# One layer of a hybrid decoder trunk on one core: sums of squares ahead of the input projection, eight input buffers, and outer products without their priority

## The chip, the cores and the metric

The kernel runs on one core of one Trainium2 chip. The metric is the device time of one execution in microseconds. Three runs of the kernel before took 1131.49, 1137.46 and 1138.11 us; their median is 1137.46 us.

## The reference

One layer works on x of 1024 tokens by 1024 channels in float32, with a conditioning vector c. What the change touches is its beginning:

```python
c_act = jax.nn.silu(c)
mod = (c_act @ w_mod[l] + b_mod[l])[:, None, :]
sh1, sc1, g1, sh2, sc2, g2 = jnp.split(mod, N_MOD, axis=-1)
h = _rms(x, norm1_w[l]) * (1 + sc1) + sh1      # x * rsqrt(mean(x*x)) * weight
proj = h @ w_in[l]
u, q, k, v = jnp.split(proj, ...)
y_ssm = _s5(u, ...)        # state-space branch: 32 groups of 16 channels, scan over positions
y_attn = _swa_sink(...)    # attention in a sliding window of 128, with sinks
x = x + g1 * (concat(norm(y_ssm), norm(y_attn)) @ w_out[l])
...                        # norm, gated MLP with a convolution of width 3, second residual
```

The state-space branch is computed in blocks of 8 positions; its discretised matrices are outer products of per-group vectors with powers of the state matrix, and they depend on the parameters alone.

## The kernel before, in words

Channels lie on the 128 partitions, in 8 tiles (k = 0 to 7) of 128 channels by 1024 tokens. A float32 product is made of three products of a fast type: each operand is split into an upper part (ScalarE, `act.copy` or `act.activation`) and a lower part (VectorE, the difference), and `mm3` (L143) adds upper x upper, upper x lower and lower x upper in one bank of PSUM. There are 8 banks.

The first projection gives u, the 512 channels of the state-space branch, with the tokens sorted by their residue j modulo 8 (T = 8): bank j takes the tokens j, j+8, ... , and its 24 products run over the 8 tiles k. The norm's factor of a token is applied only when a bank is emptied (`u_out`, L277), so the products need no norm. For each k the loop at L239 to L264

- loads x's tile (four buffers, taken in turn), a tile of the modulation weights (`emit_mod`, L178) and every second time a tile of w_in,
- reduces the modulation weights against the activated c on VectorE (L180; the trace names it CUSTOM_DVE and gives it the line 180), and forms the scale `mods` (L249),
- splits w_in's tile into the parts in `wus`, and x times the scale into `hT[k]` (tHA, tHB, tH: upper part L251 on ScalarE, lower part L252 on VectorE),
- squares x on ScalarE (L254) and adds the squares over the partitions by a product with a matrix of ones into banks 6 and 7 (L258; each shows as two records in the trace),
- adds this k's part to the six banks 0 to 5.

Behind the loop `rsqrt_mean` (L187 to L192) turns banks 6 and 7 into the norm's factor `rstd`, four instructions on ScalarE and four on VectorE; eight products with a single column, two records each, bring it from a row into a column of bank 7 (L272), and L273 copies it to `rc`. `u_out` empties banks 0 to 5, partly on VectorE, and the residues 6 and 7 are computed in banks 6 and 0 (L285 to L288).

After that come eight more tiles of modulation weights (L293), from which the shift's operand `shs` is cast and split (L296, L297). `shift_u` (L299) multiplies it with all parts of w_in. On VectorE the parameters of the state-space branch are prepared meanwhile: exponentials, sines, powers of the state matrix (PWr, PWi), and then `outer` (L415): a product with PWr, a product with PWi and their sum, for four tiles `IB` (L430; first matrix) and for `CAt` (L437; second matrix). IB is made inside `tc.high_priority(0)`. TensorE transposes IB later (L531), applies it to u (L566) and hands it to VectorE, whose scan begins with two memsets (L578). Heads of q, k and v run through `head` (L510), with weights loaded and split in `head_w` (L459).

What stands where on an engine is settled when the program is built: a list scheduler with its own estimate of times puts each instruction in its engine's order, each engine works its order off strictly, and instructions under `pin` keep the order of the text on TensorE. DMAs are issued by SyncE (SP) in order, with eight semaphores in turn.

Of the kernel before, what the change touches and what calls it, by code (L numbers as in the profile page):

```python
# [12 lines left out]
AF = mybir.ActivationFunctionType  # L13
ALU = mybir.AluOpType
ADD, SUB, MUL, MAX, MIN = ALU.add, ALU.subtract, ALU.mult, ALU.max, ALU.min
# [4 lines left out]
T = 8  # L20
# [42 lines left out]
def hymba_kernel(ctx, tc, xT, c, wmod, wu, wkvq, small, consts, relb, pq, wglu, wout, wup, wdn, out):  # L63
# [4 lines left out]
    bank = [pp.tile([128, 512], F32, name=f"bk{i}") for i in range(8)]  # L68
    SIZES = {"HA": 2048, "HB": 2048, "S16": 4128, "XQ": 4096}

    def new(tag, dt=F32):
        return pool.tile([128, SIZES.get(tag, 1024)], dt, tag=tag, name="t" + tag)
# [11 lines left out]
    def newr(tag):  # L84
        return RT(new(tag, F32R))

    vec, act, pol, sync = nc.vector, nc.scalar, nc.gpsimd, nc.sync
# [38 lines left out]
    def stt(o, a, s, b, op0, op1):  # L126
        return vec.scalar_tensor_tensor(out=o, in0=a, scalar=s, in1=b, op0=op0, op1=op1)  # L127
# [9 lines left out]
    def split(x, src, hi_eng="a", lo_eng="v"):  # L137

        hi, lo = x
        cpy(hi_eng, hi.r, src)  # L140
        tt(ENG[lo_eng], lo.r, src, hi.f, SUB)

    def mm3(o, a, b, start, stop, chain=False):  # L143

        pe.matmul(o, a[0].r, b[0].r, start=start, stop=False, skip_group_check=chain)
        pe.matmul(o, a[0].r, b[1].r, start=False, stop=False, skip_group_check=chain)
        pe.matmul(o, a[1].r, b[0].r, start=False, stop=stop, skip_group_check=chain)

    def sl(x, cols):
        return x[0][:, cols], x[1][:, cols]  # L150
# [4 lines left out]
    def half(t):  # L155
        return t[:, 0:512], t[:, 512:1024]
# [5 lines left out]
    def S(name, j=0, n=None):  # L162
        o, w = SMALL[name]
        return sm[:, o + j:o + (w if n is None else j + n)]
# [3 lines left out]
    early = new("S16")  # L168
    cact = new("X7")
# [5 lines left out]
    mod = pool.tile([128, 48], F32, name="mod")  # L175
    mods = pool.tile([128, 16], F32, name="mods")

    def emit_mod(j, st, ca):  # L178
        sync.dma_start(out=st, in_=wmod[j])
        vec.tensor_tensor_reduce(  # L180
            out=st, in0=st, in1=ca, scale=1.0, scalar=S("b_mod", j, 1), op0=MUL, op1=ADD,
            accum_out=mod[:, j:j + 1],
        )
# [42 lines left out]
    n1s = pool.tile([128, 8], F32, name="n1s")  # L226
    ts(n1s, S("n1w"), -1.0, MUL)
    hT, wus = [], []
    for k in range(8):
        if k < 2:  # L230
            t_ = newr(("HA", "HB")[k])
# [2 lines left out]
            hT.append((newr(f"H{2 * k}"), newr(f"H{2 * k + 1}")))  # L234
    wux = newr("XQ")
    jt = new("A12")[:, 0:512]
    xs = [new("X4"), new("X5"), new("X6"), early[:, 3072:4096]]
    wst = None
    for k in range(8):  # L239
        xk = xs[k % 4]  # L240
        sync.dma_start(out=xk, in_=xT[k])
        emit_mod(8 + k, early[:, (k % 3) * 1024:(k % 3 + 1) * 1024], cact)
        if k % 2 == 0:
            wst = new(("W0", "A10")[k // 2 % 2])
            sync.dma_start(out=wst, in_=wu[k // 2])
        w = half(newr(f"U{k}") if k < 4 else wux[:, (k - 4) * 1024:(k - 3) * 1024])
        wus.append(w)
        split(w, wst[:, (k % 2) * 512:(k % 2) * 512 + 512])
        stt(mods[:, k:k + 1], mod[:, 8 + k:9 + k], 1.0, n1s[:, k:k + 1], ADD, MUL)  # L249
        hi, lo = hT[k]  # L250
        act.activation(out=hi.r, in_=xk, func=AF.Identity, scale=mods[:, k:k + 1])  # L251
        stt(lo.r, xk, mods[:, k:k + 1], hi.f, MUL, SUB)  # L252
        sq = new(("A11", "A1")[k % 2])
        act.activation(out=sq, in_=xk, func=AF.Square)  # L254
        if k == 0:
            sync.dma_start(out=cn, in_=consts[:, 0:384])
        for h in range(2):
            pe.matmul(bank[6 + h], ones, sq[:, h * 512:h * 512 + 512], start=(k == 0), stop=(k == 7))  # L258
        if k == 1:
            Q12, P12, Bs_t = new("W1"), new("U5"), new("U4")  # L260
            sync.dma_start(out=Q12, in_=pq[0])
            sync.dma_start(out=P12, in_=pq[1])
        for j in range(6):
            mm3(bank[j], sl(hT[k], slice(j, 1024, T)), w, k == 0, k == 7)  # L264
    rstd = new("X6")
    rc = pool.tile([128, 8], F32, name="rc")
    rtmp = new("A11")
# [3 lines left out]
    for j in range(T):  # L271
        pe.matmul(bank[7][:, j:j + 1], rstd[0:1, j:1024:T], ones[0:1, 0:1], start=True, stop=True)  # L272
    act.copy(rc, bank[7][:, 0:8])  # L273
    U = new("S16")[:, 0:4096]
    Uv = U.rearrange("p (g d h) -> p g d h", d=8, h=16)

# [5 lines left out]

    for j in range(6):
        u_out(j, bank[j])
    for j, b in ((6, bank[6]), (7, bank[0])):  # L285
        for k in range(8):
            mm3(b, sl(hT[k], slice(j, 1024, T)), wus[k], k == 0, k == 7)
        u_out(j, b)  # L288
# [139 lines left out]
        tt(eng, o, o, tmp, ADD)  # L428

    IB = [new(f"A{5 + i}") for i in range(4)]  # L430
    hp = ctx.enter_context(ExitStack())
    hp.enter_context(tc.high_priority(0))
    for i in range(4):
        tmp = new("A10") if i == 3 else IB[i + 1]
        outer(vec, IB[i], tmp, 8 * i, 8, 8, Bb, Bsw)
    hp.close()
    CAt = [new(f"A{i}") for i in range(5)]  # L437
    for i in range(4):
        outer(vec, CAt[i][:, 0:1008], CAt[i + 1][:, 0:1008], 7 * i, 7, 9, P1, P2)
# [170 lines left out]
    for i2 in range(2):  # L610
        b = abank()
# [10 lines left out]
    for q in range(4):  # L622
        sync.dma_start(out=kd[:, 8 * q:8 * q + 8, 112:240],
                       in_=ka[32 * q:32 * q + 16, :].rearrange("p (g x) -> p g x", x=128))
# [91 lines left out]
    for i in range(8):  # L716
        b = bank[int(pick("YB", i))]
# [11 lines left out]
    for m in range(4):  # L729
        zv = zT[m].rearrange("p (c t) -> p t c", t=8)  # L730
        for q2 in range(2):
            b = sbank()
# [632 lines left out]
```

## Time and profile before

| | |
|---|---|
| runs before, us | 1131.49, 1137.46, 1138.11 |
| median | 1137.46 |
| profiled execution | 1138.01 |
| its span (first to last instruction) | 1136.1 |
| TensorE matmul busy | 1050.8 us, 92% of the span |
| VectorE busy | 928.0 us, 82% |
| ScalarE busy | 581.0 us, 51% |
| GpSimd busy | 269.0 us, 24% |
| granted TensorE clock, mean over the span | 0.962 of full |

A share of busy time is a mean over stages with different limits, so it says little about one stage. In the rows below, times are in microseconds from the start of the span; a row of the order of time gives the start, the time from the first start to the last end, the engine, the source line, the operation, the tiles out<-in, shapes and the count, and in brackets the idle time before it and what ended it. Buffer numbers are left out: tH stands for several tiles. The granted clock is the share of full speed that TensorE was given; it has two levels, 1.2 and 2.4 GHz.

### The profile page before, as it was taken

The page shows a single profiled execution, that of the slowest core. Times are in us where ns is not written, and L with a number is a line of the kernel's source. Part 1 is how long each engine was busy: PE and PEld are TensorE (multiplying, and loading weights), DVE is VectorE, ACT ScalarE, POOL GpSimd, SP SyncE. Part 2 cuts the span into 40 slices and gives each one's busy share as a digit, 9 for nine tenths or more (in the row PEclk, how much of TensorE's full clock was granted, in tenths as well). Part 3 has the DMA queues.
Part 4 walks back from the last instruction along what each step waited for, and adds up shares of the span by engine and source line. Part 5 has one row for each costly group of instructions (what it writes and reads, how often), then busy time and mean ns, then how long its engine had stood idle before and what let it go on. Part 6 is the DMA issues. An engine that isn't in the chain of part 4 may idle for free.

```text
span 1136.1 us, 13319 instructions
## 1 busy us (share of the span) xinstructions
PE 1050.8 (92%) x4692; PEld 828.1 (73%) x4692; DVE 928.0 (82%) x1493; ACT 581.0 (51%) x1008; POOL 269.0 (24%) x153
## 2 busy tenths in 40 slices
PE   6989999579989899779999999999999979989998
PEld 4877777366556577657888888888888768768876
DVE  7994899949887587888777878797778797998985
ACT  5415443578895366736544545455444554434342
POOL 0000000011233102762222223212212143353541
PEclk9989999689999899979999999999999989999999
DMA  9501516014018855222223232423123359220002
GB/s 364 224 19 38 118 50 93 1 66 139 19 47 213 258 180 155 93 93 94 92 86 112 82 128 93 154 88 112 56 93 116 125 210 382 74 93 1 1 38 112
DMA packets 48487, 128.14 MB, mean 113 GB/s; under 512 B 6146, under 2 KB 14114, under 8 KB 48419
## 3 DMA queue, kind: packets, MB, share of 16 engines
q1 hardware_dynamic: 46114, 123.09, 31.8%
q0 software_dynamic: 2304, 4.20, 2.3%
q8 instruction: 37, 0.61, 0.2%
q14 instruction: 32, 0.25, 0.1%
HBM read 105.28 MB, written 21.99 MB: 112 GB/s over the span
## 4 chain that ended last, share of the span: by engine, by line
PE 44%; DVE 11%; ACT 1%; DMA 1%; issue 1%; SPq 0%; DVEq 0%; ACTq 0%
PE bk L97 43%; DVE tA L118 2%; DVE tH L118 2%; DVE tU L118 2%; PE bk L99 1%; DVE tXQ L127 1%; DVE tX L127 1%; DVE tXQ L118 1%; DVE tX L118 1%; DVE tS L118 1%; DMA tS<-in_dram 0%; DMA tX<-xd 0%; ACT tU L133 0%; DVE tHA L118 0%; DMA tW<-in_dram 0%
## 5 line engine op out<-in xcount | busy, mean ns | idle before, releaser
L97 PE MATMUL bk<-tA,tU 128*128 128x512 f32 x516 | 128.1, 395 | 0.8 <-DVE tA L118 0.8
L97 PE MATMUL bk<-tU,tU 128*128 128x512 f32 x516 | 123.4, 391 | 4.8 <-DVE tXQ L127 2.4
L97 PEld LDWEIGHTS bk<-tU,tU 128*128 128x128 f32 x516 | 96.5, 188 | 27.4 <-issue 2.8
L97 PE MATMUL bk<-tH,tU 128*128 128x512 f32 x477 | 115.9, 392 | 0.0
L97 PEld LDWEIGHTS bk<-tA,tU 128*128 128x128 f32 x516 | 96.7, 188 | 24.2 <-DVE tA L118 1.4
L127 DVE SCALAR_TENSOR_TENSOR tX<-tH,sm,tX 128x1023 f32<-128x1023 f32 x66 | 100.2, 1519 | 7.7 <-ACT tX L1100 7.6
L97 PEld LDWEIGHTS bk<-tH,tU 128*128 128x128 f32 x477 | 89.1, 188 | 19.2
L97 PE MATMUL bk<-tA,tXQ 128*128 128x512 f32 x300 | 74.5, 395 | 1.0 <-ACT tH L1053 1.0
L97 PE MATMUL bk<-tH,tA 128*128 128x512 f32 (+1 forms) x168 | 62.5, 502 | 10.6 <-ACT tH L133 6.5
L99 PE MATMUL bk<-tH,tU 128*128 128x512 f32 x267 | 65.8, 402 | 2.3 <-DVE tU L118 2.3
L97 PEld LDWEIGHTS bk<-tA,tXQ 128*128 128x128 f32 x300 | 56.3, 188 | 14.5 <-ACT tH L1053 1.4
L133 ACT CAST tU<-tW 128x512 fp32r<-128x512 f32 (+1 forms) x67 | 47.1, 710 | 38.1 <-PE bk L97 19.9
L118 POOL TENSOR_TENSOR tU<-tW,tU 128x512 fp32r<-128x512 f32 x25 | 36.5, 1467 | 115.1 <-ACT tU L133 93.4
L118 DVE TENSOR_TENSOR tX<-tX,tX 128x512 f32<-128x512 f32 (+1 forms) x63 | 61.6, 982 | 1.7 <-DMA tX<-in_dram 0.9
L118 POOL TENSOR_TENSOR tXQ<-tW,tXQ 128x512 fp32r<-128x512 f32 x12 | 49.8, 4154 | 52.3 <-ACT tXQ L133 32.5
L99 PEld LDWEIGHTS bk<-tH,tU 128*128 128x128 f32 x267 | 51.0, 193 | 15.3 <-DVE tU L118 3.1
L118 POOL TENSOR_TENSOR tH<-tH,att 128x1024 f32<-128x1024 f32 (+1 forms) x9 | 17.0, 1890 | 176.2 <-DVE att L841 149.2
L118 POOL TENSOR_TENSOR tU<-tX,tU 128x512 fp32r<-128x512 f32 x19 | 32.9, 1736 | 85.4 <-ACT tU L133 71.3
L118 DVE TENSOR_TENSOR tU<-tW,tU 128x512 fp32r<-128x512 f32 (+2 forms) x43 | 37.8, 881 | 18.2 <-ACT tU L133 18.2
L97 PE MATMUL bk<-tXQ,tH 128*128 128x256 f32 (+2 forms) x224 | 50.2, 368 | 1.6 <-DVE att L829 1.6
L118 DVE TENSOR_TENSOR tU<-tX,tU 128x512 fp32r<-128x512 f32 x39 | 31.3, 808 | 23.4 <-ACT tU L133 23.4
L97 PEld LDWEIGHTS bk<-tXQ,tH 128*128 128x128 f32 x224 | 44.5, 268 | 8.2 <-DVE att L829 4.3
(351 smaller groups left out, 2423.4 us busy)
## 6 DMA issues: line engine op xcount, KB each, us to landing
tW<-in_dram SPq DMA_DIRECT2D x49, 512.0 KB, 3.3
tX<-in_dram SPq DMA_DIRECT2D x47, 512.0 KB, 3.3
tS<-in_dram SPq DMA_DIRECT2D x30, 512.0 KB, 7.1
gd<-tX SPq DMA_DIRECT2D x22, 512.0 KB, 2.9
tA<-in_dram SPq DMA_DIRECT2D x12, 512.0 KB, 10.0
tH<-in_dram SPq DMA_DIRECT2D x12, 512.0 KB, 5.0
tH<-gd SPq DMA_DIRECT2D x8, 512.0 KB, 4.4
tA<-gd SPq DMA_DIRECT2D x8, 512.0 KB, 9.8
```

The source lines that it names most:

```text
L97: return f(*a, **k)
L99: i = f(*a, **k)
L118: return eng.tensor_tensor(out=o, in0=a, in1=b, op=op)
L127: return vec.scalar_tensor_tensor(out=o, in0=a, scalar=s, in1=b, op0=op0, op1=op1)
L133: act.copy(o, i)
```

## The change

- x's tiles get eight buffers (the spaces A0, A2, A3, A4, X4, X5, the fourth quarter of `early`, and A8) in place of four.
- The first loop now only loads, squares and adds the squares; the modulation weights and w_in of k = 0 to 2 are loaded in it (`fill`). The norm's factor, the single-column products and `rc` follow at once in the text, and the loop over reductions, splits and products comes behind them.
- Residue 7 takes bank 7 in place of bank 0.
- IB's outer products lose their high priority.

```diff
--- before.py
+++ after.py
@@ -234,34 +234,27 @@
             hT.append((newr(f"H{2 * k}"), newr(f"H{2 * k + 1}")))
     wux = newr("XQ")
     jt = new("A12")[:, 0:512]
-    xs = [new("X4"), new("X5"), new("X6"), early[:, 3072:4096]]
-    wst = None
+    xs = [new(t_) for t_ in ("A0", "A2", "A3", "A4", "X4", "X5")] + [early[:, 3072:4096], new("A8")]
+    wst, wmt = {}, {}
+
+    def fill(k):
+
+        wmt[k] = early[:, (k % 3) * 1024:(k % 3 + 1) * 1024]
+        sync.dma_start(out=wmt[k], in_=wmod[8 + k])
+        if k % 2 == 0:
+            wst[k // 2] = new(("W0", "A10")[k // 2 % 2])
+            sync.dma_start(out=wst[k // 2], in_=wu[k // 2])
+
     for k in range(8):
-        xk = xs[k % 4]
-        sync.dma_start(out=xk, in_=xT[k])
-        emit_mod(8 + k, early[:, (k % 3) * 1024:(k % 3 + 1) * 1024], cact)
-        if k % 2 == 0:
-            wst = new(("W0", "A10")[k // 2 % 2])
-            sync.dma_start(out=wst, in_=wu[k // 2])
-        w = half(newr(f"U{k}") if k < 4 else wux[:, (k - 4) * 1024:(k - 3) * 1024])
-        wus.append(w)
-        split(w, wst[:, (k % 2) * 512:(k % 2) * 512 + 512])
-        stt(mods[:, k:k + 1], mod[:, 8 + k:9 + k], 1.0, n1s[:, k:k + 1], ADD, MUL)
-        hi, lo = hT[k]
-        act.activation(out=hi.r, in_=xk, func=AF.Identity, scale=mods[:, k:k + 1])
-        stt(lo.r, xk, mods[:, k:k + 1], hi.f, MUL, SUB)
-        sq = new(("A11", "A1")[k % 2])
-        act.activation(out=sq, in_=xk, func=AF.Square)
+        sync.dma_start(out=xs[k], in_=xT[k])
         if k == 0:
             sync.dma_start(out=cn, in_=consts[:, 0:384])
+        if k < 3:
+            fill(k)
+        sq = new(("A11", "A1")[k % 2])
+        act.activation(out=sq, in_=xs[k], func=AF.Square)
         for h in range(2):
             pe.matmul(bank[6 + h], ones, sq[:, h * 512:h * 512 + 512], start=(k == 0), stop=(k == 7))
-        if k == 1:
-            Q12, P12, Bs_t = new("W1"), new("U5"), new("U4")
-            sync.dma_start(out=Q12, in_=pq[0])
-            sync.dma_start(out=P12, in_=pq[1])
-        for j in range(6):
-            mm3(bank[j], sl(hT[k], slice(j, 1024, T)), w, k == 0, k == 7)
     rstd = new("X6")
     rc = pool.tile([128, 8], F32, name="rc")
     rtmp = new("A11")
@@ -271,6 +264,25 @@
     for j in range(T):
         pe.matmul(bank[7][:, j:j + 1], rstd[0:1, j:1024:T], ones[0:1, 0:1], start=True, stop=True)
     act.copy(rc, bank[7][:, 0:8])
+    for k in range(8):
+        xk = xs[k]
+        if k > 2:
+            fill(k)
+        vec.tensor_tensor_reduce(out=wmt[k], in0=wmt[k], in1=cact, scale=1.0, scalar=S("b_mod", 8 + k, 1), op0=MUL, op1=ADD,
+                                 accum_out=mod[:, 8 + k:9 + k])
+        w = half(newr(f"U{k}") if k < 4 else wux[:, (k - 4) * 1024:(k - 3) * 1024])
+        wus.append(w)
+        split(w, wst[k // 2][:, (k % 2) * 512:(k % 2) * 512 + 512])
+        stt(mods[:, k:k + 1], mod[:, 8 + k:9 + k], 1.0, n1s[:, k:k + 1], ADD, MUL)
+        hi, lo = hT[k]
+        act.activation(out=hi.r, in_=xk, func=AF.Identity, scale=mods[:, k:k + 1])
+        stt(lo.r, xk, mods[:, k:k + 1], hi.f, MUL, SUB)
+        if k == 1:
+            Q12, P12, Bs_t = new("W1"), new("U5"), new("U4")
+            sync.dma_start(out=Q12, in_=pq[0])
+            sync.dma_start(out=P12, in_=pq[1])
+        for j in range(6):
+            mm3(bank[j], sl(hT[k], slice(j, 1024, T)), w, k == 0, k == 7)
     U = new("S16")[:, 0:4096]
     Uv = U.rearrange("p (g d h) -> p g d h", d=8, h=16)
 
@@ -282,7 +294,7 @@
 
     for j in range(6):
         u_out(j, bank[j])
-    for j, b in ((6, bank[6]), (7, bank[0])):
+    for j, b in ((6, bank[6]), (7, bank[7])):
         for k in range(8):
             mm3(b, sl(hT[k], slice(j, 1024, T)), wus[k], k == 0, k == 7)
         u_out(j, b)
@@ -428,12 +440,9 @@
         tt(eng, o, o, tmp, ADD)
 
     IB = [new(f"A{5 + i}") for i in range(4)]
-    hp = ctx.enter_context(ExitStack())
-    hp.enter_context(tc.high_priority(0))
     for i in range(4):
         tmp = new("A10") if i == 3 else IB[i + 1]
         outer(vec, IB[i], tmp, 8 * i, 8, 8, Bb, Bsw)
-    hp.close()
     CAt = [new(f"A{i}") for i in range(5)]
     for i in range(4):
         outer(vec, CAt[i][:, 0:1008], CAt[i + 1][:, 0:1008], 7 * i, 7, 9, P1, P2)
```

What the scheduler makes of it is seen in the engines' orders. On TensorE, at the end of the six banks, before: bk_69 is bank 6, bk_70 bank 7, bk_63 bank 0; cn is the tile of constants, tX_362 the norm's factor, and tU and tXQ hold the parts of w_in.

```order
L97 MATMUL bk_69<-tXQ,tH_95 128x512 x2
L97 MATMUL bk_69<-tXQ,tH_96 128x512
L97 MATMUL bk_69<-tXQ,tH_97 128x512 x2
L97 MATMUL bk_69<-tXQ,tH_98 128x512
L97 MATMUL bk_70<-cn,tX_362 128x1 x8
L97 MATMUL bk_63<-tU_109,tHA 128x512 x3
L97 MATMUL bk_63<-tU_141,tHB 128x512 x3
L97 MATMUL bk_63<-tU_179,tH_87 128x512 x2
```

On TensorE after, from the last product of k=3 in bank 6 on (tH_91 and tH_92 are the upper and lower part of k=4):

```order
L97 MATMUL bk_69<-tU_258,tH_90 128x512
L97 MATMUL bk_63<-tXQ,tH_91 128x512 x2
L97 MATMUL bk_64<-tXQ,tH_91 128x512 x2
L97 MATMUL bk_65<-tXQ,tH_91 128x512 x2
L97 MATMUL bk_66<-tXQ,tH_91 128x512 x2
L97 MATMUL bk_67<-tXQ,tH_91 128x512 x2
L97 MATMUL bk_68<-tXQ,tH_91 128x512 x2
L97 MATMUL bk_69<-tXQ,tH_91 128x512 x2
L97 MATMUL bk_63<-tXQ,tH_92 128x512
```

Residue 6 (bank 6) now runs along with the six banks, and the single-column products and residue 7 in bank 7 follow further down in the same run. The order's first 52 rows hold all the sums of squares.

On VectorE before, around the lower part of the last operand, tH_98 (tU_152, tU_153 and Bbt are vectors of the state-space branch; tA_562 and the tiles like it are parts of outer products; ISA is a reduction of modulation weights):

```order
L127 SCALAR_TENSOR_TENSOR tH_96<-tX_103,mods,tH_95 128x1024
L118 TENSOR_TENSOR PWi<-PWi,tU_153 128x32x4
L180 ISA tX_439,mod<-tX_439,tX_75,sm 128x1024
L180 ISA mod 128x1
L118 TENSOR_TENSOR ep<-ep 128x16
L127 SCALAR_TENSOR_TENSOR tH_98<-tS_74,mods,tH_97 128x1024
L118 TENSOR_TENSOR tA_562<-tU_153,PWi 128x1024
L118 TENSOR_TENSOR tA_579<-tU_152,PWi 128x1008
L118 TENSOR_TENSOR tA_580<-tU_152,PWi 128x1008
```

On VectorE after, the rows ahead of the lower part of k=4, tH_92, in two pieces (tA_158 and tX_156 are the norm's):

```order
L118 TENSOR_TENSOR tA_566<-tU_210,PWi 128x1024
L118 TENSOR_TENSOR tA_567<-tU_210,PWi 128x1024
L118 TENSOR_TENSOR tA_583<-tU_209,PWi 128x1008
L118 TENSOR_TENSOR tA_584<-tU_209,PWi 128x1008
L118 TENSOR_TENSOR tA_585<-tU_209,PWi 128x1008
L127 SCALAR_TENSOR_TENSOR tA_158<-bk_70,tA_158 128x512
L127 SCALAR_TENSOR_TENSOR mods<-mod,n1s 128x1
L180 ISA tA_445,mod<-tA_445,tX_75,sm 128x1024
L180 ISA mod 128x1
L118 TENSOR_TENSOR tA_586<-tU_209,PWi 128x1008
```

The second piece follows directly:

```order
L127 SCALAR_TENSOR_TENSOR tX_156<-tA_158,tX_156 128x512
L127 SCALAR_TENSOR_TENSOR mods<-mod,n1s 128x1
L271 ISA tS_74,mod<-tS_74,tX_75,sm 128x1024
L271 ISA mod 128x1
L661 COPY ep<-PWi 64x16
L118 TENSOR_TENSOR tA_578<-tU_210,PWi 128x1024
L127 SCALAR_TENSOR_TENSOR tH_92<-tX_105,mods,tH_91 128x1024
L118 TENSOR_TENSOR tA_565<-tA_565,tA_566 128x1024
L118 TENSOR_TENSOR tA_582<-tA_582,tA_583 128x1008
```

Seven products with PWi that stood behind the last operand now stand ahead of the operand of k=4, together with steps of the norm.

On TensorE before, where the first head's weights (tU_639, tU_640) meet the shift's operand and the first transposes of IB (tA_561) stand ahead of the second head's products (tU_1001 and tU_1002 are the parts of its weights):

```order
L99 MATMUL bk_68<-tU_639,shs 2x128
L99 MATMUL bk_68<-tU_640,shs 2x128
L99 MATMUL bk_67<-cn,tA_561 128x128 x4
L97 MATMUL bk_69<-cn,brow 128x1
L99 MATMUL bk_68<-cn,tA_561 128x128 x4
L97 MATMUL bk_64<-tHA,tU_1001 128x512 x2
L99 MATMUL bk_69<-cn,tA_562 128x128 x4
```

And after (tU_643 and tU_644; tA_565; tU_1005 and tU_1006):

```order
L99 MATMUL bk_68<-tU_643,shs 2x128
L99 MATMUL bk_68<-tU_644,shs 2x128
L99 MATMUL bk_67<-cn,tA_565 128x128 x4
L97 MATMUL bk_64<-tHA,tU_1005 128x512 x2
L97 MATMUL bk_64<-tHA,tU_1006 128x512
L97 MATMUL bk_64<-tHB,tU_1005 128x512 x2
L97 MATMUL bk_64<-tHB,tU_1006 128x512
```

Of the transposes of IB only the first group still stands ahead of the second head's products; brow and the others come behind them.

## Rows read from the trace of the kernel before

**Rows 1.** Stretches: length, busy per engine (instructions), granted clock, DMA share, GB/s.
```profile
13.60:62.10 48.50, 48.48 (x174) 41.35 (x172) 48.15 (x118) 22.22 (x28) 0.00 (x0) 1.00 0.66 259
66.50:74.05 7.55, 7.51 (x24) 6.65 (x24) 7.55 (x10) 0.00 (x0) 0.00 (x0) 0.78 0.22 69
74.05:79.00 4.95, 3.98 (x18) 3.89 (x17) 4.58 (x11) 1.12 (x4) 0.00 (x0) 0.77 0.02 3
79.00:86.90 7.90, 7.90 (x25) 7.00 (x26) 7.90 (x11) 2.25 (x4) 0.00 (x0) 0.71 0.00 0
130.00:200.00 70.00, 68.10 (x353) 52.51 (x345) 67.88 (x135) 27.88 (x42) 0.00 (x0) 1.00 0.44 86
200.00:300.00 100.00, 81.18 (x391) 59.86 (x392) 78.28 (x192) 71.42 (x156) 11.89 (x7) 0.83 0.17 58
```
**Rows 2.** Order of time on TensorE, 13 to 95 us.
```profile
13.64 4.24 PE L97 MATMUL bk<-tU,tHA 128*128 128x512 f32 x12
...
40.47 9.36 PE L97 MATMUL bk<-tXQ,tH 128*128 128x512 f32 x36
49.67 3.60 PE L97 MATMUL bk<-tA,cn 128*128 128x512 f32 x8
52.70 9.38 PE L97 MATMUL bk<-tXQ,tH 128*128 128x512 f32 x36
66.54 1.67 PE L97 MATMUL bk<-tU,tHA 128*128 128x512 f32 x3 [4.47 <-DVE tA L127]
...
74.05 3.96 PE L97 MATMUL bk<-cn,tX 1*128 1x1 f32 x16
78.99 1.67 PE L97 MATMUL bk<-tU,tHA 128*128 128x512 f32 x3 [0.97 <-ACT tS L279]
...
86.89 2.94 PE L99 MATMUL bk<-tU,shs 128*128 128x512 f32 x12
...
94.78 0.38 PE L97 MATMUL bk<-cn,brow 2*128 2x1 f32 x2 [0.76 <-DVE brow L471]
```
**Rows 3.** Order of time on VectorE, 54 to 79 us.
```profile
54.00 1.28 DVE L127 SCALAR_TENSOR_TENSOR tH<-tS,mods,tH 128x1024 fp32r<-128x1024 f32 x1
55.20 9.10 DVE L118 TENSOR_TENSOR tA<-tU,PWi 128x1024 f32<-128x1024 f32 x8
...
64.59 1.28 DVE L180 CUSTOM_DVE_ANT_0 tX<-tX,tX,sm 128x1024 f32<-128x1024 f32 x1
...
65.80 1.28 DVE L127 SCALAR_TENSOR_TENSOR tA<-bk,tA 128x512 f32<-128x512 f32 x2
...
76.44 0.16 DVE L118 TENSOR_TENSOR shs<-mod,shs 128x8 fp32r<-128x8 f32 x1
...
78.25 1.41 DVE L122 TENSOR_SCALAR tS<-bk,rc 128x512 f32<-128x512 f32 x2 [0.36 <-ACT rc L273]
```
**Rows 4.** Order of time, all engines, around the second head's weights.
```profile
88.87 1.22 DVE L118 TENSOR_TENSOR tU<-tW,tU 128x1024 fp32r<-128x1024 f32 x1 [1.07 <-ACT tU L133]
...
90.12 7.20 SPq L461 DMA_DIRECT2D tW<-in_dram  x2
...
94.54 1.05 ACT L133 CAST tU<-tW 128x1024 fp32r<-128x1024 f32 x1
...
95.76 1.20 DVE L118 TENSOR_TENSOR tU<-tW,tU 128x1024 fp32r<-128x1024 f32 x1
...
97.44 0.48 PE L97 MATMUL bk<-tHA,tU 128*128 128x512 f32 x1
```
**Rows 5.** Waits of VectorE, 0 to 130 us: total, times, longest.
```profile
DVE tS L578 <- PE bk L99: 10.0, 1, 10.0
```
**Rows 6.** Waits of TensorE, 200 to 300 us.
```profile
PE bk L97 <- ACT tX L493: 6.4, 3, 4.8
PE bk L97 <- DVE tX L127: 3.9, 1, 3.9
```

## The prediction

> **What bounds the kernel now.** I read the stretches first, then the order of time on TensorE and VectorE, then who waited for whom. The stretch from TensorE's first product to the end of the sixth bank, 13.60 to 62.10 us, shows both engines full: TensorE 48.48 of 48.50 us, VectorE 48.15 [rows 1]. So TensorE waits for no operand and no load in there, and VectorE has no room either. What can be gained lies behind it. After the six banks TensorE stands 4.47 us until VectorE has read banks 6 and 7 for the norm (tA L127), runs the seventh residue, turns the norm's row into a column in sixteen one-column records (3.96 us), and stands 0.97 us until ScalarE has emptied bank 0 [rows 2]. The clock is worth reading there: 1.00 in the long stretch, but a mean of 0.78, 0.77 and 0.71 in the three stretches from 66.50 to 86.90 us [rows 1]; the levels are 1.2 and 2.4 GHz, so a mean of 0.78 over 7.55 us is 3.3 us at the lower one. Everything behind hangs on TensorE: VectorE then waits 10.0 us for it in one piece ahead of the scan (tS L578) [rows 5].
>
> **Paces.** 36 products take from 40.47 to 49.67 us: 0.2556 us each. Eight records of the square sums (two residues' worth of k) take from there to 52.70 us: 1.51 us per k. The seventh residue takes 66.54 to 74.05 us, 7.51 us, where 24 x 0.2556 = 6.13 would do: 1.38 lost to the lower clock after the wait. The eighth takes 78.99 to 86.89 us, 7.90: 1.77 lost [rows 2]. On VectorE an outer product's step costs 9.10 / 8 = 1.14 us, a step of the norm 0.64, a reduction of the modulation weights 1.21 by the start of the next row, and the lower part of an operand 1.20 (the 1.28 shown less the 0.08 that overlaps the next) [rows 3].
>
> **What the change removes.** Both waits and both clock losses, if the two last residues ran on in the same rush: 4.47 + 0.97 + 1.38 + 1.77 = 8.6 us. Nothing else goes: the same 192 products, 32 sum records and 16 one-column records are issued, and the same VectorE rows.
>
> **What it adds: a later operand.** The norm's chain and the outer products are now ahead of operands in VectorE's queue. The order of VectorE shows it: ahead of the lower part of k=4 (tH_92) now stand seven of the outer products' steps with PWi, and before the first of these came only behind the last operand of all (tH_98). I set the rows ahead of the new tH_92 against the rows that stood ahead of the old tH_98, which started at 54.00 us [rows 3]. Added: 7 outer steps (8.0), 3 norm steps (1.9), a copy (0.2). No longer ahead: 3 lower parts (3.6), 3 reductions (3.6). Net +2.9: tH_92 starts at 56.9 and is ready at 58.1 us. This holds because VectorE was packed up to there in the profile, so a queue's sum is its time.
>
> **When TensorE wants it.** By the new order 98 products and seven k of square sums stand between the first product and tH_92. From 13.64 us: 98 x 0.2556 = 25.0, 7 x 1.51 = 10.6, and about 1.1 for the first twelve (4.24 shown for 3.07) [rows 2]: 50.4 us. The earlier arrival of the constants might save some tenths at the start; I credit none, since the wait swallows them. TensorE then stands some 7.7 us, where before it stood 5.4 in two pieces.
>
> **From there to the shift.** After tH_92 come 94 products (24.0) and the sixteen one-column records (3.96): 86.1 us at the full clock. What the clock costs after a wait of 7.7 us is not shown; the nearest rows are the wait of 4.47 us (1.38) and the one-column run (1.77), and both causes are still there, so I take 3.2; bounds 1.4 (one of them) and 5.1 (all of the stretch at the lower clock lost half its time: 3.3 + 2.3 + 4.6 = 10.2 us, halved). So the eighth residue ends at 89.3 us, against 86.89: +2.4.
>
> The Trainium skill's page "TensorE: Matmul & The Clock Gate", in its Terms, prices a throttled stretch at its length times the share of pulses held back, which is that upper 5.1. The trace does not agree for these stretches: they lost 3.2 us, since TensorE stood still in part of them. By the page the sum would be 1.9 us more.
>
> **The shift's operand.** shs was ready at 76.5 us and nobody waited. Ahead of it now stand 8 more steps of outer products (9.1), two evacuations by VectorE (0.7 each), and small rows (0.4): 87.3 us [rows 3]. But the first evacuation needs bank 1 finished: 52 products after tH_92, the one-column run and the clock, 58.1 + 13.3 + 4.0 + 3.2 = 78.6 us, while VectorE reaches it 11.4 us ahead of shs, at 75.9. It waits 2.7 us, and what is queued behind it, four reductions, outer steps and shs, moves with it: shs at 90.0. TensorE begins the shift with the upper parts, so I charge 0.5: shift at 89.8, +2.9. Bounds: 0 and 0.7.
>
> **The heads' weights behind it.** The second head's weights are loaded when VectorE has split the first head's: 88.87 + 1.2, issued at 90.12, and their split is ready at 96.9 us, 6.8 us later [rows 4]. Now the first split is queued 2.9 us behind shs: done at 94.1, the second at 99.9 (5.8 us, since the cast has no copy ahead of it in ScalarE's queue now). TensorE's own work would bring it there at 89.8 + 5.6 (shift) + 1.4 + 0.5 = 97.3. Wait 2.6, less the 0.76 for brow that stood there before [rows 2]: +1.9. Bounds 0 (other products fill it) and 2.9. The transposes, which were filler there, now stand behind it, as the last order fence shows.
>
> **Sum.** 2.4 + 0.5 + 1.9 = +4.8 us. The profiled execution took 1138.01 us (span 1136.1), 0.55 above the median of the three runs. 1138.0 + 4.8 = 1142.8. Past the shift the 10.0 us that VectorE waits [rows 5] show that its outer products are not late for the scan, and that TensorE's delay passes straight on; from 130 to 200 us TensorE is 97% busy [rows 1], so little is caught up.
>
> **The rivals.** *A, the operands come in time.* Eight buffers let every load of x run ahead, the banks run on without a break, and the two waits are gone. For it: no load and no operand was late from 13.60 to 62.10 us. Against it: the place of tH_92 behind seven outer steps in a queue that had no gap. Price: -8.6, with the one-column run's 1.77 still paid -6.8: 1131.2 us. The Trainium skill, "Trainium Kernel Development and Optimization", Best Practices, asks for double buffers so that loads overlap work, which is this rival's reason; the trace bears it out only so far that loads were overlapped already, so buffers alone give nothing here.
>
> *B, a later stage pays as well.* TensorE's order also changes among the transposes and products of attention, which run between 200 and 300 us, where it is busy only 81.18 of 100 us [rows 1] and its longest waits are 4.8 us for ScalarE (tX L493) and 3.9 for VectorE (tX L127) [rows 6]. If the new order brings each of these once more, that is 4.8 + 3.9 on top of +4.8: 1151.5 us. It decides from 6.6 us of new waits there (with +4.8 past 1%). For it: those stages hang on single results. Against: most of the rows there stand as before.
>
> *C, the delay is taken up.* Between the shift and the scan TensorE waits for small results in several places and filler moves; if the pinned stretch swallows the delay, the time stays: 1138.0 us. Against: +1.9 of new waits lie exactly there.
>
> *D, the change does nothing to the order that counts.* Excluded by the order itself.
>
> **How the numbers follow.** About 1% (11.4 us) is what a measurement of this kernel can tell from no change. Forecast 0.50, its own range 1139 to 1146 from the bounds of the clock, shift and weights; A 0.16; C 0.18; B 0.12; 0.04 for what I do not see. Of A some tail is past 1% faster (below 1126.1): 0.05. Slower past 1% (above 1148.8): B and a little: 0.14. The range that leaves out 2 in 10 goes from A's time to near B's: 1131 to 1150.
>
> **What would show it.** Right: a wait of TensorE of 7 to 8 us for VectorE at tH (L127), ending near 58 us, in a stretch that before had none; the granted clock at the lower level right after it; no waits any more ahead of the seventh and eighth residue; shs near 87 to 90 us; tS L578 starting at 112 to 116 us instead of 109.8. Wrong: a gapless TensorE from 13 to about 79 us (then A), tS L578 at 109 to 110 us (C), or a distance to it that stays below 5 us while the end moves by over 11 (B). If tH_92 is ready before 52 us, the set-off of rows is wrong and with it the forecast.

## The result, and the profile after

| | before | after |
|---|---|---|
| runs, us | 1131.49, 1136.03, 1137.46, 1138.11 | 1146.3, 1148.85, 1149.35, 1149.38 |
| median | 1136.74 | 1149.1 |
| ratio of the runs, 95% interval | | 1.0113 [1.0082, 1.0144] |
| span of the profiled execution | 1136.1 | 1147.6 |
| VectorE at the scan's memset | 109.80 | 116.74 |

The change costs 12.4 us, 1.1%. The forecast was 1142.8 with a range of 1131 to 1150: the sign and the range held, the size, +4.8 us, was less than half of what came. The scan begins 6.9 us later; the rest, some 5 us, arises behind it.

The order of time on TensorE in the changed kernel answers to [rows 2] (start, time to the last end, engine, line, operation, tiles, shapes, count, idle time before and what ended it):

```profile
57.73 7.08 PE L97 MATMUL bk<-tXQ,tH 128*128 128x512 f32 x21 [7.87 <-DVE tH L127]
64.73 3.96 PE L97 MATMUL bk<-cn,tX 1*128 1x1 f32 x16
68.62 13.64 PE L97 MATMUL bk<-tXQ,tH 128*128 128x512 f32 x49
82.10 0.92 PE L97 MATMUL bk<-tU,tHA 128*128 128x512 f32 x3
...
89.03 3.04 PE L99 MATMUL bk<-tU,shs 128*128 128x512 f32 x12 [0.86 <-ACT shs L308]
...
97.58 0.73 PE L97 MATMUL bk<-tHA,tU 128*128 128x512 f32 x2 [1.34 <-ACT tU L133]
98.84 0.50 PE L97 MATMUL bk<-tHA,tU 128*128 128x512 f32 x1 [0.53 <-DVE tU L118]
...
100.42 5.37 PE L97 MATMUL bk<-tH,tU 128*128 128x512 f32 x18
...
107.40 1.60 PE L99 MATMUL bk<-cn,tS 128*128 128x128 f32 x12
109.39 0.66 PE L99 MATMUL bk<-cn,tS 128*128 128x128 f32 x4 [0.39 <-ACT tA L557]
110.42 0.66 PE L99 MATMUL bk<-cn,tA 128*128 128x128 f32 x4 [0.38 <-ACT tA L557]
```

One wait of 7.87 us stands where there were 4.47 and 0.97. Behind it the residues 6 and 7 follow without a gap. From 106.03 us the transposes run bare, that is without products between them, and from 109 us on TensorE waits for ScalarE's copy (L557) between one group and the next: seven times, six of them 0.38 or 0.39 us, the last 0.51.

VectorE in the changed kernel, answering to [rows 3, 5]:

```profile
56.40 1.27 DVE L127 SCALAR_TENSOR_TENSOR tH<-tX,mods,tH 128x1024 fp32r<-128x1024 f32 x1
...
89.00 0.17 DVE L118 TENSOR_TENSOR shs<-mod,shs 128x8 fp32r<-128x8 f32 x1 [0.18 <-ACT shs L308]
...
116.74 0.07 DVE L587 MEMSET tS<- 128x16 f32 x1 [10.45 <-PE bk L99]
```

The first row is the lower part of k=4 (tH_92): ready at 57.7 us.

Stretches of the changed kernel, answering to [rows 1] (stretch, its length, busy time and instructions by engine, granted clock, DMA share, GB/s):

```profile
core 0: us, PE busy (x) PEld busy (x) DVE busy (x) ACT busy (x) POOL busy (x), PEclk, DMA share, GB/s
49.80:57.70 7.90, 0.06 (x1) 0.00 (x0) 7.90 (x14) 2.30 (x2) 0.00 (x0) 0.82 0.00 0
57.70:64.70 7.00, 6.97 (x21) 6.04 (x21) 6.94 (x9) 1.15 (x1) 0.00 (x0) 0.72 0.46 150
64.70:88.20 23.50, 23.46 (x90) 22.50 (x89) 21.89 (x32) 3.60 (x6) 0.00 (x0) 0.93 0.26 90
90.00:118.00 28.00, 23.34 (x137) 17.77 (x138) 8.82 (x33) 13.86 (x42) 0.00 (x0) 0.94 0.11 38
130.00:200.00 70.00, 69.67 (x412) 53.51 (x411) 67.66 (x135) 28.41 (x44) 0.00 (x0) 1.00 0.35 78
```

VectorE is packed while TensorE stands: 7.90 of 7.90 us. The clock, in stretches of TensorE alone (stretch, its length, TensorE's busy time and instructions, granted clock, DMA share, GB/s):

```profile
54.83:61.66 6.83, 3.93 (x9) 0.50 0.24 78
61.66:68.49 6.83, 6.83 (x29) 1.00 0.32 98
68.49:71.90 3.41, 3.41 (x9) 0.50 0.38 138
99.21:102.62 3.41, 3.41 (x10) 0.50 0.44 154
```

It stands at its lower level three times: in the long wait and just behind it, behind the sixteen one-column records, and behind the wait for the second head's weights (the rows at 97.58 and 98.84 us).

Who waited for whom on TensorE from 200 to 300 us, answering to [rows 6] (engine, line, waited for: us in total, times, the longest):

```profile
PE bk L97 <- ACT tX L502: 6.4, 3, 4.7
PE bk L97 <- DVE tX L127: 3.9, 1, 3.9
```

They are the waits of before, no more and no less.

### The profile page after: what moved, and what is told of

Read it like the earlier page. It is cut to its first block, busy times and chain, and to the rows that moved or that the text cites. A ratio compares the mean times of both kernels' runs of the same rounds, so it can differ in the third digit from the quotient of the medians.

```text
span 1147.6 us, 13307 instructions
## 1 busy us (share of the span) xinstructions
PE 1057.2 (92%) x4692; PEld 827.1 (72%) x4692; DVE 927.3 (81%) x1493; ACT 581.6 (51%) x1008; POOL 268.3 (23%) x153
## 4 chain that ended last, share of the span: by engine, by line
PE 45%; DVE 11%; issue 1%; ACT 1%; DMA 1%; DVEq 0%; ACTq 0%
PE bk L97 44%; DVE tH L118 2%; DVE tA L118 2%; DVE tU L118 2%; DVE tX L127 1%; PE bk L99 1%; DVE tXQ L127 1%; DVE tX L118 1%; DVE tXQ L118 1%; DVE tS L118 1%; DVE tHA L118 0%; DMA tX<-xd 0%; DMA tW<-in_dram 0%; DVE tW L127 0%; DVE tW L118 0%
## 5 line engine op out<-in xcount | busy, mean ns | idle before, releaser
L97 PE MATMUL bk<-tH,tU 128*128 128x512 f32 x477 | 119.0, 399 | 0.0
L99 PE MATMUL bk<-tH,tU 128*128 128x512 f32 x267 | 68.1, 409 | 4.0 <-DVE tU L118 3.8
L97 PEld LDWEIGHTS bk<-tA,tXQ 128*128 128x128 f32 x300 | 56.3, 188 | 14.5 <-ACT tH L1062 1.6
```

The costliest lines, as they stand in the source:

```text
L97: return f(*a, **k)
L99: i = f(*a, **k)
```

## The experiments

Two questions were open: is it VectorE's order that costs the time ahead of the scan, and where do the other 5 us come from? Theory 1 has it that all real loss lies ahead of the scan and that the rest is what executions of one program differ by; theory 2 that norm, buffers and loads cost it, or a later stage. Each time below is the median of its runs, the ratio is to runs of the kernel before on the same chip (medians 1135.2, 1135.5 and 1136.15 us in the three groups of runs).

**Both kernels once more.** No edit.

> The kernel before once more, for its profile alone: how far do two executions of one program lie apart, and where? Theory 1 (the change loses some 7 us ahead of the scan, and the 4.6 us by which its profile falls back after 320 us, in rows that stand in the same order in both kernels, is what executions of one program differ by): this profile differs from the first one by under 0.5 us up to the scan's memset at 109.8 us, and by 3 to 6 us somewhere behind 500 us. Theory 2 (a later stage really loses in the change): it lies within 1 us of the first one at every landmark.

> The changed kernel once more, for its profile alone. Theory 1: the scan's memset again near 116.7 us (7 us behind the kernel before), TensorE's wait for the lower part of k=4 again 7.9 us, and the distance to the kernel before at the end anywhere from 5 to 13 us. Theory 2: the same 11 to 12 us at the end, built up at the same places after 320 us.

Measured: 1135.68 us for before, 1150.95 for after, one run each. Their memsets stand at 111.61 and 117.44 us, and TensorE's wait for the lower part of k=4 is 7.8 us again. At the scan before lies 1.8 us behind its first profile, more than the 0.5 expected, and stays so up to 200 us; by 280 us it has made up all but 0.2, and from 380 us on it is 4 us ahead: two executions of one program do differ in the middle, by several microseconds. But after's distance, 5.8 us at the scan, grew to 14.5 us at 400 us and stayed there. Variation alone does not give that.

**The changed kernel with its outer products behind the last operand.** The early norm, the eight buffers and the loads stay. The block that holds IB's products back now ends behind those of CAt.

```diff
-        stt(lo.r, xk, mods[:, k:k + 1], hi.f, MUL, SUB)
+        last_lo = stt(lo.r, xk, mods[:, k:k + 1], hi.f, MUL, SUB)
...
+    hp = ExitStack()
+    hp.enter_context(tc.issue_after(last_lo.ins))
     IB = [new(f"A{5 + i}") for i in range(4)]
```

> The changed kernel with all outer products held behind the lower part of the last operand (k=7): early norm, eight buffers and the order of loads stay. Theory 1 (the seven outer steps ahead of the lower part of k=4 in VectorE's queue cost it): without them (7 x 1.14 = 8.0 us) the lower part is ready at 57.7 - 8.0 = 49.7 us, TensorE wants it at 49.9, so the wait of 7.87 is gone, with it up to 1.6 us of lower clock behind it; the outer steps come back ahead of shs, whose 2 us then wait; the scan's memset comes 5 to 8 us earlier than 116.7, and the time is 1140 to 1144. Theory 2 (the early norm, the buffers or the loads cost it, the outer products are only where the wait is booked): the wait moves to another operand, the memset stays within 1.5 us of 116.7 and the time at 1147 to 1151.

Measured: 1145.12 us, 1.0086 [1.0062, 1.011]. TensorE's order of time, and the memset on VectorE:

```profile
45.71 11.43 PE L97 MATMUL bk<-tXQ,tH 128*128 128x512 f32 x46
57.07 3.96 PE L97 MATMUL bk<-cn,tX 1*128 1x1 f32 x16
...
79.60 3.04 PE L99 MATMUL bk<-tU,shs 128*128 128x512 f32 x12 [0.86 <-ACT shs L308]
```

```profile
109.92 0.07 DVE L590 MEMSET tS<- 128x16 f32 x1 [12.05 <-PE bk L99]
```

The 7.87 us are gone, the shift starts 9.4 us earlier than in the changed kernel and the memset comes 6.8 us earlier, as theory 1 said. And yet only 4 us reach the end: the distance to before (second profile) goes from -1.7 us at 280 us to +8.1 at 410. The time lies between the two expectations, and neither theory holds as it stands.

**The kernel before with its outer products behind the norm.** One change of the order ahead of the scan, nothing else (here too the block ends behind CAt's products):

```diff
-        rsqrt_mean(rstd[:, hs], rtmp[:, hs], bank[6 + h], D)
+        nrm = rsqrt_mean(rstd[:, hs], rtmp[:, hs], bank[6 + h], D)
...
-    hp.enter_context(tc.high_priority(0))
+    hp.enter_context(tc.issue_after(nrm.ins))
```

> The kernel before with nothing but its outer products held behind the last step of the norm (they stood ahead of it in VectorE's queue, some eight steps of 1.14 us): no early norm, four buffers, old loads. Theory 1 (what counts in this stretch is only where the outer products stand in VectorE's order): the sixth bank ends at 62.1 us as before, VectorE reads banks 6 and 7 at once, so the 4.47 us wait becomes about 1 and the eighth residue's 0.97 goes; with 1 to 3 us of clock back the shift starts at 79 to 83 us instead of 86.9, the scan's memset comes 3 to 6 us earlier than 109.8, and the time is 1131 to 1134, better than both kernels. Theory 2 (these waits are hidden further on, by what the scan waits for on VectorE): memset within 1.5 us of 109.8, time 1135 to 1138.

Measured: 1142.76 us, 1.0069 [1.0049, 1.0089]: slower, outside both expectations. The memset is at 107.11 us, both waits ahead of residues 6 and 7 are gone and the shift starts at 79.16; at 200 us this kernel is 4.5 us ahead of before (second profile), at 400 us 5.0 us behind it. Here is what differs there. The buffer of the last modulation weights comes free later, seen by the first transfer into it on SP's queue, of before (second profile) and of this kernel:

```profile
341.26 0.34 SPq L894 DMA_DIRECT2D tS<-cad  x1
```

```profile
349.12 0.34 SPq L894 DMA_DIRECT2D tS<-cad  x1
```

and VectorE, which reduces these sixteen weights of 512 KB each, waits longer for them (who waited for whom on VectorE, 300 to 400 us, before and then this kernel):

```profile
DVE tS L180 <- DMA tS<-in_dram: 8.0, 4, 4.1
```

```profile
DVE tS L180 <- DMA tS<-in_dram: 17.0, 7, 5.2
```

(In before's first profile this sum is 13.9 us, so part of the difference is from execution to execution.)

The stretches of this kernel (columns as above) show fewer transfers ahead of 340 us; before (second profile) moved 47 GB/s in the first of them and 241 in the second:

```profile
300.00:340.00 40.00, 31.68 (x130) 17.49 (x129) 34.88 (x99) 36.67 (x97) 10.56 (x5) 0.91 0.08 27
340.00:400.00 60.00, 51.17 (x199) 35.73 (x198) 39.02 (x64) 24.88 (x47) 14.99 (x14) 0.91 0.82 236
```

Compared row by row, the built orders of all these kernels agree again soon behind the scan, and then differ once more between some 220 and 410 us, in attention, gated branch and output projection, whose text nobody touched (two of them also swap single rows near 510 us): the scheduler chooses by its modelled times, and these moved. That is theory 3: the change pays twice. Its rival, theory 4: the stage loses because it is reached at another time, whatever its order.

**The late order set by hand.** For these runs the order of each engine from the scan's start to some 410 us is written out as a list and forced, taken from one kernel and put on the other:

```diff
+    for runs in LATE.values():
...
+                    tc.add_manual_dep(i, prev.name, mybir.DependencyInfo(
+                        mybir.DependencyClass.NoSync, mybir.DependencyReason.DATA), reason="late order")
+                prev = i
```

These edges hold the issue order on one engine and add no wait between engines. Between the two lists 59 of TensorE's 1170 instructions change places, the fewest that turn one into the other. A kernel with its own order written out was not run, so what the edges alone do to the time is not shown.

> The changed kernel, with the order of every engine from behind the scan's start up to some 410 us (attention, gated branch, projection) set by hand to that of the kernel before; the first 110 us are the changed kernel's own. Theory 3 (the change costs twice: some 6 us at the scan's start, because operands stand behind outer products, and some 7 to 9 us between 300 and 400 us, because the scheduler, whose choices there follow from its modelled times, gave another order of attention and projection): only the first part is left, the scan's memset at 116 to 118 us, the distance to the kernel before stays at 6 to 7 us through 320 and 400 us, time 1140 to 1143. Theory 4 (that stage loses whatever its order, because it is reached at another time, by its transfers or the clock): the distance grows there to 13 to 15 us as it did in the changed kernel, time 1147 to 1151.

> The mirror image: the kernel before in its first 110 us, with the changed kernel's order from there to some 410 us. Theory 3: memset at 109.8 to 111.6 us as before, no distance up to 310 us, then 7 to 9 us lost up to 400 us, the last unit of attention 12 us or more later than at 356 to 359 us; time 1142 to 1145. Theory 4: the stage is reached at the old time, so nothing is lost, time 1134 to 1138.

> The kernel before with its outer products behind the norm (4.5 us earlier at the scan, then 9.7 us lost between 320 and 380 us, in the run with the scheduler's own order), now with the late order of the kernel before. Theory 3: the 4.5 us are kept to the end, time 1129 to 1133, better than both kernels. Theory 4: the same loss again, time 1140 to 1144.

> The changed kernel with its outer products behind the lower part of the last operand (1.7 us earlier at the scan than the kernel before, then 9.5 us lost between 320 and 380 us), now with the late order of the kernel before. Theory 3: 1132 to 1136, within 0.3% of the kernel before, so that early norm and eight buffers by themselves give 0 to 3 us. Theory 4: 1143 to 1147.

Measured, medians in us:

| ahead of the scan as in | late order of before | late order of after |
|---|---|---|
| before | 1135.5 | 1140.95, 1.0042 [1.0016, 1.0067] |
| after | 1143.36, 1.0062 [1.0041, 1.0083] | 1149.1 |
| before, outer products behind the norm | 1131.41, 0.9959 [0.9942, 0.9977] | |
| after, outer products behind the last operand | 1134.92, 0.9995 [0.9981, 1.0009] | |

The two halves add up: 0.62% for the first part and 0.42% for the late order (7.9 and 5.5 us), 1.04% together, against 1.13% for the change. Theory 3 stands. Two sizes lie just outside what was expected: the first expectation's upper end was 1143, the second's lower end 1142 (theory 4 had at most 1138 there), and the ten runs of the second spread from 1133.2 to 1148.8, so that its 0.42% may be 0.16 to 0.67. In the two lower rows the late order weighs more: 1.1 points (1.0069 against 0.9959) and 0.9 (1.0086 against 0.9995), by the other late orders that the scheduler had given those two kernels. The late order has a mark that goes with it and not with the first part, TensorE's waits from 300 to 420 us (after; before's first part with after's late order; after's first part with before's late order):

```profile
PE bk L97 <- DVE tHA L118: 6.4, 1, 6.4
PE bk L97 <- DVE tA L118: 2.7, 1, 2.7
```

```profile
PE bk L106 <- DVE tHA L127: 7.0, 1, 7.0
PE bk L106 <- DVE tA L127: 2.7, 1, 2.7
```

```profile
PE bk L106 <- DVE tHA L127: 2.7, 1, 2.7
```

tHA is the lower part of a tile of the output weights (the lines are nine further down where the list stands in the file). In before the same row reads 0.7 us in one profile and 2.6 in the other.

The third kernel beats both: before's program with its outer products behind the norm and its own late order, 0.4% faster than before. The fourth says what the early norm and eight buffers are worth when their operands come in time: nothing, between -0.2 and +0.1%.

**Where in the late order.** Only the last piece, from the last unit of attention on, is set to the order of before; no other edit than a shorter list.

> The changed kernel with only the last piece of the late order set to that of the kernel before: from the last unit of attention on (some 340 us), where the changed kernel lets 24 products of the projection go ahead of it on TensorE and two reductions of modulation weights on VectorE. Theory 5 (the late loss sits in that piece: the last unit ends at 376 us instead of 356 to 360): most of the 5 to 6 us come back, time 1143 to 1146. Theory 6 (the loss is spread over the units between 240 and 340 us, in many small waits): time 1147 to 1150.

Measured: 1146.3 us, 1.0094 [1.0067, 1.0121]. By the ratios it closes 0.19 of the 0.51 points between the whole change (1.0113) and the run with all of the late order put back (1.0062): the time falls between the two expectations, and neither theory holds in its pure form. By the medians, each less its kernel before, it is 2.2 of 4.5 us. So the last piece is a third to a half of it, but a step of 0.2 points lies inside the intervals of the runs, and the size is open. Of the two waits above, the one for tHA falls to 2.9 us here and the 2.7 us for tA stay. The last unit's reciprocal on VectorE, in the changed kernel (second profile) and here:

```profile
375.95 0.17 DVE L850 RECIPROCAL att<-att 128x4 f32<-128x4 f32 x1
```

```profile
366.36 0.17 DVE L859 RECIPROCAL att<-att 128x4 f32<-128x4 f32 x1
```

**The products beside the transposes.** The second half of the second head, 24 products, is held behind the scan's start, on after's and on before's first part, all with the late order of before. (The expectations call it the first head's; its products are those that wait for the second head's weights at 97.58 us.)

```diff
     with pe.pin(True):
-        for _ in range(17):
+        for _ in range(26):
             next(h0, None)
```

> The changed kernel with the late order of the kernel before (1143.4 us, memset at 116.9 us, in the run without the next edit), and the first head's second half held in its fixed place behind the scan's start, so that its 24 products no longer run ahead of the transposes. Theory 3 (of the early loss, some 4.8 us arise between shift and memset, because those 24 products, 6 us, now run first and the transposes then wait bare for ScalarE): the memset comes 3 to 5 us earlier, at 112 to 114 us, and since the 24 products have to run later beside the scan, where TensorE has some room, 2 to 4 us are left at the end: 1139 to 1142. Rival: the transposes are paced by ScalarE's copies anyway, the memset stays at 116 to 117 us and the time at 1142 to 1145.

> The kernel before with its outer products behind the norm and its late order kept (1131.4 us, memset at 107.0 us), and the first head's second half held behind the scan's start as well. If the scan's start sets the end: memset 2 to 4 us earlier, at 103 to 105 us, time 1128 to 1131. If the 24 products moved behind the memset are paid there in full (TensorE is 97% busy from 130 to 200 us): 1130 to 1134.

> The kernel before with its late order kept and only the first head's second half held behind the scan's start (outer products where they were). If the scan's start sets the end: memset 2 to 5 us earlier than 109.8 to 111.6 us, time 1131 to 1134. If the products are paid behind it: 1134 to 1137, no change.

Measured: on after's first part 1143.93 us, 1.0067 [1.004, 1.0093]; on before's with the outer products behind the norm 1132.72, 0.9977 [0.9959, 0.9995]; on before's own 1133.7, 0.9979 [0.9962, 0.9997]. The first brings its memset from 116.89 to 113.02 us as expected, and nothing of it reaches the end (1143.36 without the edit), where the rival was right in the time alone. Its stretch from 118 to 200 us has no gap on TensorE:

```profile
118.00:200.00 82.00, 82.00 (x528) 63.62 (x525) 74.03 (x143) 31.01 (x48) 0.00 (x0) 1.00 0.37 80
```

TensorE takes up behind the memset what it did not do ahead of it, and without the edit it was full there already, 81.65 of 82.00 us. In after's first part the scan's start is a landmark, not the bound. The second, expected at 1128 to 1131 if the scan's start set the end, has its memset at 104.67 us as expected and gained nothing over 1131.41. The third lies in the range of the scan's start as the bound (1131 to 1134), its memset at 107.79 us: with its interval just clear of 1 it may gain 0.2%, and before did have 1.9 and 1.2 us of idle TensorE from 118 to 200 us in its two profiles. What bounds this stretch in general is not shown.

## Why the prediction was right, and where it fell short

*The wait.* Predicted: the lower part of k=4 starts at 56.9 us and is ready at 58.1, wanted at 50.4, a wait of 7.7. Measured: 56.40, 57.7, 49.86, 7.87. Setting the rows ahead of it off against the rows that stood ahead of another instruction in a packed queue was enough; the queue was packed again (43.55 of 44.10 us from 13.60 to 57.70). That it is VectorE's order and not the norm, the buffers or the loads is shown by the run in which the outer products alone were moved away: TensorE then runs through to 78.7 us. Which part of the change sent the outer products ahead, the two loops or the lost priority of IB's, was not run by itself.

*The clock.* 3.2 us taken. The 21 products behind the wait took 7.00 us and the next 49 took 13.48 (68.62 to 82.10). At the full clock products start 0.2445 us apart (from 41.11 to 49.67 us in the kernel before; 0.244 from 72 to 82 us here), so 21 would take 5.13 and 49 would take 11.98: 3.4 us lost. The prediction's pace of 0.2556 was too long: it holds 0.4 us of changing over from the square sums. By it the 94 products were charged 1.0 us too much, and the clock loss of the kernel before was read as 3.2 us where it is 1.64 + 2.03 = 3.7. The term came out near the mark, and the products ended at 88.2 us instead of 89.3. The Trainium skill, "TensorE: Matmul & The Clock Gate", Terms, would charge the length times the share held back: 7.00 x 0.28 + 23.50 x 0.07 = 3.6 us as an estimate. The trace agrees to 0.2 us here; in the kernel before the same rule gives 5.1 for 3.7, since the clock was low in part of the wait and of the one-column records too.

*The shift.* shs predicted at 90.0, measured 89.00; the shift at 89.8, measured 89.03, +2.1 us instead of +2.9. VectorE's wait for the first bank was 1.6 us instead of 2.7.

*From the shift to the scan: mis-sized.* The term was +1.9 for the second head's weights. That wait came to 1.34 + 0.53 less 0.76, +1.1. But the stretch from the shift to the memset is 27.7 us against 22.9 in [rows 2, 5], in every profile of the two first parts (27.7, 27.7, 27.6 and 27.7 us; 22.9, 22.9 and 22.9): +4.8. TensorE in it, before and after (columns as in the stretches of TensorE alone):

```profile
86.89:109.80 22.91, 20.97 (x132) 1.00 0.14 47
89.03:116.74 27.71, 23.56 (x131) 0.94 0.11 39
```

It stands still 4.15 us instead of 1.94: the 1.1, and 1.1 more for ScalarE's copies, since bare transposes go at the pace of these, 1.03 us for four. And the same work runs 2.6 us longer. Some 1.5 of that is the clock, at its lower level from 99.2 to 102.6 us where before shows 1.00 throughout: eight products start 0.43 us apart instead of 0.23. The rest of the 2.6 is not assigned. The prediction priced the wait alone; it said that the transposes now stand behind the products and gave that no price, and it put the clock behind this wait at nothing. With it the memset comes 6.9 us later, outside the 112 to 116 us that the prediction named.

*The step that failed: rival B.* "Against: most of the rows there stand as before", with a chance of 0.12 and the waits of 4.8 and 3.9 us that would come once more. Both waits are the same after the change. The later stage paid all the same, behind 300 us instead of between 200 and 300, because few moved rows are enough: 59 of TensorE's 1170 instructions stand elsewhere in the late order, and that order costs 5.5 us on its own (0.16 to 0.67%). Shown by the four corners. Where in this order the time is lost was narrowed to the last piece, with the last unit behind the projection, for a third to a half of it; the rest is open.

*The other rivals.* A's condition, operands in time, can be made true, and its first half then holds: the shift starts at 79.6 us, 7.3 earlier than in [rows 2], within A's 6.8 to 8.6. But the memset comes no earlier than 109.92 and 108.47 us in the two kernels made so, since VectorE has to do the outer products sometime, and is busy 19.90 of the 20 us from 70 to 90 us in the second. Nothing reaches the end. C fell with the memset. D was excluded by the order, rightly for the change as a whole; what the lost priority does alone was not run.

*The range.* The forecast's own range, 1139 to 1146, missed. That 1149.1 lies within 1131 to 1150 is luck in part: the upper end was drawn near the time of rival B, and B's waits did not come.

*The sum.* Against the mean of the profiles with before's first part at the memset (109.80, 111.61, 110.48) the changed first part (116.74, 117.44, 116.89, 116.27) is 6.2 us later; 5.5 come from the late order, and 1.5 from what the last section shows. That makes 13.2 us; measured were 12.4, with an interval of 9.3 to 16.4 (0.82 to 1.44% of 1136.74).

## What to carry to other kernels

On an in-order engine with no gap, an early instruction is paid for by what stands behind it: read which rows come to stand ahead of the next operand that TensorE wants, and add them up. Where a scheduler orders by modelled times, a change at the beginning can reorder a stage far behind it, so compare the built orders to the end, and hold the late order fixed before judging the early change: here the late order hid a gain of 0.4% and made a loss of 7.9 us one of 12.4. A gain at a landmark need not reach the end: where TensorE is full behind it, work moved behind the landmark is only paid later. And a forecast that adds a wait on TensorE has to ask for the clock behind it: in the changed kernel it fell behind waits of 7.87 and of 1.34 + 0.53 us, and not behind the one of 0.86 us ahead of the shift.

## What was not expected of the hardware

A stretch of some 380 us in the gated MLP, with row for row the same order on every engine, takes a different time in the kernels with the changed loops. From one cast of ScalarE to another, of before (second profile), and of the changed first part with before's late order:

```profile
547.42 0.62 ACT L133 CAST tXQ<-tX 128x512 fp32r<-128x512 f32 x1 [0.15 <-PE bk L97]
...
927.43 0.62 ACT L133 CAST tU<-tA 128x512 fp32r<-128x512 f32 x1
```

```profile
553.73 0.62 ACT L142 CAST tXQ<-tX 128x512 fp32r<-128x512 f32 x1 [0.19 <-PE bk L106]
...
935.27 0.62 ACT L142 CAST tU<-tA 128x512 fp32r<-128x512 f32 x1
```

380.01 us and 381.54 us. In all seven profiles with before's loops ahead of the scan it is 379.99 to 380.02 us, in all seven with the changed loops 381.52 to 381.54. The granted clock is 0.99 in both. The difference sits in the products of certain pairs of tiles (line, engine, operation, tiles, shapes, count, busy us, mean ns of one, idle us before), in the same two profiles:

```profile
L97 PE MATMUL bk<-tH,tU 128*128 128x512 f32 x288 | 69.5, 391 | 0.0
L97 PE MATMUL bk<-tA,tXQ 128*128 128x512 f32 x253 | 63.0, 395 | 0.0
```

```profile
L106 PE MATMUL bk<-tH,tU 128*128 128x512 f32 x288 | 70.9, 395 | 0.0
L106 PE MATMUL bk<-tA,tXQ 128*128 128x512 f32 x253 | 62.5, 393 | 0.0
```

From start to start a product of tH and tU takes 228.4 ns in all seven profiles of the one kind and 233.0 or 233.1 in all seven of the other; those of tHA and tHB with tU slow down by 5 and 7 ns, those of tA and tXQ gain 2. Counted over the stretch that makes the 1.5 us. So it goes with the tiles that a product reads. Whether it is something that carries over from the beginning, or where the tiles lie, since the changed loops name their buffers in another order, was not tried. The 1.5 us take back most of the 2.2 us by which the memset of the fourth kernel of the table (108.47) is ahead of the mean of the three with before's first part (110.63).

The other surprise is the spread: before's first part with after's late order ran from 1133.2 to 1148.8 us in ten runs, the changed kernel, with the same late order, from 1146.3 to 1150.95 in five. Which of the transfers in the crowded stretch from 340 to 400 us comes first may differ from run to run; that was not tested.
